# Layer 0's opening blocks in a hand-written order on four engines

## The chip, the cores and the metric

One core of one Trainium2 chip runs the whole program in one launch. The metric is the device time of one execution in microseconds (us). Matmuls run on TensorE (PE), elementwise work on VectorE (DVE), ScalarE (ACT) and GpSimd (POOL). Loads are issued by SyncE (SP) and carried out by the core's 16 DMA engines.

## The reference

Two layers of a bidirectional encoder over 2048 tokens of 1024 channels, then a final RMSNorm. What bears on the change is how a layer begins:

```python
h = rms_norm(x, norm_w[l])                 # x: (1, 2048, 1024), float32
proj = h @ w_in                            # one combined projection
qkv, z_a, a_lg, b_lg, cf_val, cf_glu, z_b, gate_lg = jnp.split(proj, pts, axis=-1)
qkv = jax.nn.silu(depthwise_conv_centred(qkv, qkv_conv_w))   # width 5
# q, k, v: 4 heads of 128; l2-normalised q and k; a_lg, b_lg: decay and write strength
# chunked delta rule forward and backward, gated norm, w_dn_out
# conformer branch: GLU, conv of width 31, layer norm, w_cf_out
# merge by gates, w_out, residual add
```

For the first layer, `rms_norm(x)` must be computed from the input itself: the sum of squares of each token over 1024 channels, its reciprocal root, and the scaled x.

## The kernel before, in words

Everything is kept channel-major: a tile has 128 channels on the partitions and tokens along the free axis. The 1024 channels are 8 tiles (index k, `KD`), and the 2048 tokens are four blocks of 512 (`NB`), two to a half. A product is made at high precision from rounded parts: an operand is split into a high half (`hi`, rounded, by ScalarE) and a low half (`lo`, the rest, by VectorE; `split`, L157 and L158). A column tile of 128 output channels over one block takes, for each k, three matmuls of 128x512: w high by h high, w high by h low, w low by h high (`dense_steps`, L174 to L176). The 16 columns for decay and write strength ("scalar tile") are stacked as high and low in one stationary tile `wab` and take two matmuls for each k (L408, L409).

The code is written for a planner: instructions are recorded in program order with their data dependencies, and the planner then chooses an order for each engine, and on which buffers an instruction waits, from its own model of times. In two cases the order is written by hand instead: `bind(start)` chains all instructions recorded since `start` on PE, ACT, DVE and POOL, each to the one before it on its engine. Before the change this is done for the delta rule's stage. DMA issues on SyncE are never bound.

Buffers come from pools of few slots: `big` (4), `mid` (3), `hm` (5), staging tiles `st` of 128x512 (3), weights `whi` and `wlo` (2 each), raw weights `wraw` (2 pieces of 4 k), PSUM `pd` (3 banks) and `pz` (5 banks). A new tile in a pool waits until an older one has been used up.

The opening of layer 0 is `head(0)`. It makes the scalar tile and the column tiles of k and q for head 0 (`conv_tiles([4, 0], block)`), block by block, while the generator `first_norm` is pulled along in small steps (`need`, `step_lead`). `first_norm` does, for each block: load 8 tiles of x, square them on ScalarE (L308), add them up (L310; VectorE for block 0, GpSimd for the others), sum over the partitions by four matmuls of one column (`token_sum`, L200), a reciprocal root by 11 small VectorE operations (L190 to L196), spread the factor over the partitions with diagonals and matmuls (`spread`, L206 and L208), and then, for each k, scale x (L327) and split it into the halves of h (L157, L158). Block 3 is loaded twice, the first time through staging tiles for the squares alone. Each column tile is copied from PSUM into a padded tile `cin` (L529), and after two blocks a depthwise convolution of width 5 runs over it: one ScalarE operation (L551) and four VectorE operations (L553) on some 1022 tokens, then SiLU (L540). After the opening come the scalars' chain (`scalars`), the v tile of head 0 (`conv_tiles([8])`), the conformer's tiles and the later heads.

Of the kernel before, what the change touches and what calls it, by code (L numbers as in the profile page):

```python
# [6 lines left out]
F32 = mybir.dt.float32  # L7
# [7 lines left out]
P = 128  # L15
# [20 lines left out]
R2 = 3.7  # L36
BIG = -1.0e30
# [39 lines left out]
class Trunk:  # L77
# [82 lines left out]
    def weight(self, src, kk):  # L160
        hi = self.pw.tile([P, KD, P], F32R, tag="whi", bufs=2, name="whi")[:, 0:kk, :]
        lo = self.pw.tile([P, KD, P], F32R, tag="wlo", bufs=2, name="wlo")[:, 0:kk, :]
        for k in range(0, kk, 4):
            raw = self.pw.tile([P, 4, P], F32, tag="wraw", bufs=2, name="wraw")
            self.load(raw, src[:, k:k + 4, :])
            self.split(hi[:, k:k + 4, :], lo[:, k:k + 4, :], raw)
# [35 lines left out]

    def spread(self, ps, r, n):
# [24 lines left out]
    def normalise(self, half, xn, r, wcol):  # L228
        nc = self.nc
        hs = [self.big([P, 2, KD, NB], F32R, f"h{2 * half + b}") for b in range(2)]  # L230
# [6 lines left out]
        for k in range(KD):  # L237
            for b in range(2):
# [4 lines left out]
                self.split(hs[b][:, 0, k, :], hs[b][:, 1, k, :], t)  # L243
# [4 lines left out]
    def run(self):  # L248
        tc, nc, a = self.tc, self.nc, self.a
        with tc.tile_pool(name="cst", bufs=1) as cst, \  # L250
# [26 lines left out]
            self.ready = 0  # L277
            h = [None] * 4
            self.h = h
            self.scalar_weights(0)  # L280
            self.lead = self.first_norm(a)
            next(self.lead)
# [4 lines left out]
    def first_norm(self, a):  # L287
        nc = self.nc
        stage = self.big([P, 2, KD, NB], F32, "x0")
        for blk in range(4):  # L290
            half, b = divmod(blk, 2)
            self.h[blk] = self.big([P, 2, KD, NB], F32R, f"h{blk}")
            hi, lo = self.h[blk][:, 0], self.h[blk][:, 1]
            src = [a["x"][k, :, blk * NB:(blk + 1) * NB] for k in range(KD)]
            if half == 0:
                x = [stage[:, b, k, :] for k in range(KD)]
            elif b == 0:
                x = self.first_tiles()
            if blk < 3:
                for k in range(KD):  # L300
                    self.load(x[k], src[k])
            acc = self.st("sqa")
            eng = nc.gpsimd if blk else nc.vector
            for k in range(KD):
                sq = self.st("sq0") if k else acc
                if blk == 3:
                    self.load(sq, src[k])
                nc.scalar.activation(sq, sq if blk == 3 else x[k], AF.Square)  # L308
                if k:
                    eng.tensor_tensor(out=acc, in0=acc, in1=sq, op=ALU.add)  # L310
            yield
            ps = self.pz()
            self.token_sum(ps, acc, 4)
            v = self.sm(4, "nv")
            r = self.sm(4, "nr")
            nc.vector.tensor_scalar(out=v, in0=ps[:, 0:4], scalar1=1.0 / D, scalar2=EPS,
                                    op0=ALU.mult, op1=ALU.add)
            self.rsqrt(r, v, 4)
            yield
            if blk == 3:  # L320
                x = self.first_tiles()
                for k in range(KD):
                    self.load(x[k], src[k])
            pr = self.pz()
            self.spread(pr, r, 4)
            for k in range(KD):
                nc.vector.scalar_tensor_tensor(out=x[k], in0=x[k], scalar=self.vec[:, V_NW + k:V_NW + k + 1], in1=pr,  # L327
                                               op0=ALU.mult, op1=ALU.mult)
                self.split(hi[:, k, :], lo[:, k, :], x[k])
                if k == KD - 1:  # L330
                    self.ready = blk + 1
                if k % 2:
                    yield

    def first_tiles(self):
        t = self.mid("x0m")
# [6 lines left out]
    def need(self, blk):  # L343
        while self.ready <= blk:
            next(self.lead)
# [1027 lines left out]
```

## Time and profile before

| | us |
|---|---|
| median of 3 runs | 3189.29 (3188.14 to 3192.9) |
| the profiled execution's own time | 3187.47 |
| its span | 3185.7 |
| TensorE busy | 3090.6 (97%) |
| VectorE busy | 2398.4 (75%) |
| ScalarE busy | 1385.3 (43%) |
| GpSimd busy | 302.3 (9%) |
| mean granted TensorE clock | 0.993 |

The span runs from the first to the last instruction of the profiled execution, and times in the timeline count from its start. In a row of the timeline the first number is the start, the second the duration, then engine, line, operation, output<-inputs and the count of merged instructions; in brackets stands how long the engine had been idle, and what released it. In a table of windows the columns are the window, its length, busy time and instruction counts of PE, PE's weight loads, DVE, ACT and POOL, the granted clock, the DMA engines' busy share and GB/s. A matmul's recorded duration overlaps the next one's, so the pace is read from start to start.

### The profile page before, as it was taken

What the parts mean: (1) busy time and instruction counts of PE and PEld (TensorE: products, weight loads), DVE (VectorE), ACT (ScalarE), POOL (GpSimd) and SP (SyncE); (2) the same over time, 40 slices, a digit from 0 to 9 for tenths busy, and PEclk for the clock granted to TensorE, in tenths of its full rate; (3) what the DMA queues carried; (4) which work ended last, traced back from release to release, by engine and by line L of the source; (5) the groups of instructions that cost most, each with busy time, mean ns of one, the idle gap of its engine ahead of it and who ended that gap; (6) DMA issues with size and microseconds to landing.
All of it is one profiled execution on the core that took longest, in us unless ns stands there. A gap on an engine that the chain in (4) does not pass through costs nothing. (4 is left out here: it accounts for less than half of the span.)

```text
span 3185.7 us, 51259 instructions
## 1 busy us (share of the span) xinstructions
PE 3090.6 (97%) x19110; PEld 2705.8 (85%) x19110; DVE 2398.4 (75%) x4409; ACT 1385.3 (43%) x3104; POOL 302.3 (9%) x297
## 2 busy tenths in 40 slices
PE   6999999999999999999999999999999999999997
PEld 5788888888889998787888888888888999878786
DVE  7789898987646697745676989898955567867655
ACT  5625151522444466533345242425234445655332
POOL 3000000000122231000000000000002222200000
PEclk9999999999999999999999999999999999999999
DMA  4323222334687886654413131414357777855634
GB/s 141 90 96 93 87 93 87 93 112 133 206 288 247 258 267 208 198 185 133 135 53 101 66 120 60 120 60 123 117 186 261 243 252 255 283 182 192 204 126 146
DMA packets 427545, 501.70 MB, mean 157 GB/s; under 512 B 96224, under 2 KB 260704, under 8 KB 427296
## 3 DMA queue, kind: packets, MB, share of 16 engines
q1 hardware_dynamic: 354544, 388.58, 39.2%
q10 hardware_dynamic: 64688, 80.09, 7.3%
q0 software_dynamic: 8064, 29.76, 2.5%
q8 instruction: 150, 2.46, 0.3%
q14 instruction: 99, 0.81, 0.1%
HBM read 342.74 MB, written 155.58 MB: 156 GB/s over the span
## 5 line engine op out<-in xcount | busy, mean ns | idle before, releaser
L174 PE MATMUL pd<-h,whi 128*128 128x512 f32 x2816 | 1092.1, 388 | 0.0
L176 PE MATMUL pd<-h,wlo 128*128 128x512 f32 x2816 | 1070.4, 380 | 1.9 <-DVE wlo L158 1.9
L175 PE MATMUL pd<-h,whi 128*128 128x512 f32 x2816 | 1070.9, 380 | 0.0
L728 DVE SCALAR_TENSOR_TENSOR cacc<-gp,vec,cacc 128x1009 f32<-128x1009 f32 (+1 forms) x480 | 614.3, 1280 | 37.5 <-ACT cacc L726 34.3
L176 PEld LDWEIGHTS pd<-h,wlo 128*128 128x128 f32 x2816 | 533.8, 190 | 79.3 <-DVE wlo L158 3.5
L174 PEld LDWEIGHTS pd<-h,whi 128*128 128x128 f32 x2816 | 534.0, 190 | 79.0 <-issue 1.4
L175 PEld LDWEIGHTS pd<-h,whi 128*128 128x128 f32 x2816 | 534.5, 190 | 72.4 <-issue 1.9
L157 ACT ACTIVATE whi<-wraw 128x512 fp32r<-128x512 f32 x400 | 242.7, 623 | 473.2 <-PE pd L175 335.9
L158 DVE TENSOR_TENSOR wlo<-wraw,whi 128x512 fp32r<-128x512 f32 x400 | 275.0, 701 | 142.1 <-ACT whi L157 141.8
L553 DVE SCALAR_TENSOR_TENSOR acc<-cin,vec,acc 128x1022 f32<-128x1022 f32 (+1 forms) x192 | 246.5, 1299 | 14.4 <-ACT acc L551 13.2
L176 PE MATMUL pd<-yhi,wlo 128*128 128x512 f32 x512 | 194.9, 381 | 3.8 <-DVE wlo L158 3.7
L174 PE MATMUL pd<-yhi,whi 128*128 128x512 f32 x512 | 194.6, 380 | 0.9 <-ACT whi L157 0.9
L175 PE MATMUL pd<-ylo,whi 128*128 128x512 f32 x512 | 194.0, 379 | 0.0
L808 ACT ACTIVATE go<-pd,vec 128x512 f32<-128x512 f32 x128 | 87.1, 680 | 147.9 <-PE pd L176 138.2
L529 ACT ACTIVATE cin<-pd 128x512 f32<-128x512 f32 x96 | 57.0, 594 | 154.7 <-PE pd L176 154.6
L176 PEld LDWEIGHTS pd<-yhi,wlo 128*128 128x128 f32 x512 | 96.8, 189 | 19.9 <-DVE wlo L158 6.4
L740 ACT ACTIVATE ao<-pd 128x512 f32<-128x512 f32 x64 | 38.3, 598 | 170.0 <-PE pd L176 169.9
L174 PEld LDWEIGHTS pd<-yhi,whi 128*128 128x128 f32 x512 | 96.8, 189 | 15.4 <-ACT whi L157 2.0
L175 PEld LDWEIGHTS pd<-ylo,whi 128*128 128x128 f32 x512 | 96.8, 189 | 13.6
L174 PE MATMUL pd<-uop,whi 128*128 128x512 f32 x256 | 101.0, 395 | 6.6 <-ACT whi L157 6.5
L176 PE MATMUL pd<-uop,wlo 128*128 128x512 f32 x256 | 99.1, 387 | 2.3 <-DVE wlo L158 1.4
L175 PE MATMUL pd<-gop,whi 128*128 128x512 f32 x256 | 97.7, 381 | 3.0 <-DVE gop L158 3.0
(297 smaller groups left out, 4754.9 us busy)
## 6 DMA issues: line engine op xcount, KB each, us to landing
wraw<-w_in SPq DMA_DIRECT2D x240, 256.0 KB, 3.3
gt<-go ACTq DMA_DIRECT2D x128, 256.0 KB, 3.6
dl<-gr SPq DMA_DIRECT2D x128, 256.0 KB, 5.2
dl<-kq SPq DMA_DIRECT2D x64, 512.0 KB, 6.1
dl<-kv SPq DMA_DIRECT2D x64, 512.0 KB, 5.8
wraw<-w_out SPq DMA_DIRECT2D x96, 256.0 KB, 3.0
kq<-acc SPq DMA_DIRECT2D x16, 1024.0 KB, 5.5
gr<-go ACTq DMA_DIRECT2D x64, 256.0 KB, 2.2
```

The lines of the kernel that those rows point to most:

```text
L157: self.nc.scalar.activation(hi, src, AF.Copy)
L158: self.nc.vector.tensor_tensor(out=lo, in0=src, in1=hi.bitcast(F32), op=ALU.subtract)
L174: mm(ps, whi[:, k, :], xhi, start=k == 0, stop=False)
L175: mm(ps, whi[:, k, :], xlo, start=False, stop=False)
L176: mm(ps, wlo[:, k, :], xhi, start=False, stop=k == kk - 1)
L529: nc.scalar.activation(cut(t[:, o + b * NB:o + (b + 1) * NB]), sort(ps), AF.Copy)
L553: self.nc.vector.scalar_tensor_tensor(out=out, in0=t[:, k:k + n], scalar=wc(k), in1=out, op0=ALU.mult, op1=ALU.add)
L728: self.nc.vector.scalar_tensor_tensor(out=acc, in0=t[:, k:k + n], scalar=wc(k), in1=acc, op0=ALU.mult, op1=ALU.add)
L740: nc.scalar.activation(cut(o), sort(ps), func)
L808: nc.scalar.activation(cut(o), sort(ps), AF.Identity, bias=self.vec[:, V_GB + j:V_GB + j + 1])
```

## The change

A new method `opening()` takes the place of `first_norm`, `scalar_tiles` and `conv_tiles([4, 0])` in layer 0; layer 1 is as before. All 32 tiles of x are loaded at once into tiles of their own, with the weights of k and q between them. The weights and `wab` are rounded on VectorE instead of ScalarE. The squares of blocks 0 and 1 are summed in PSUM, by token sums that accumulate (`token_add`): in block 0, pairs are added on VectorE first for k up to 5, and tiles 6 and 7 go straight to TensorE; in block 1 all eight go straight to TensorE. Squares of blocks 2 and 3 are added on GpSimd. The squares of later blocks are dealt out one for each k (`FIRST`). For each k of a block, x is scaled and split, and then the two matmuls of the scalar tile and the three of k and of q follow. The first-half convolutions are laid into block 3, one step for each k. All of it up to the last transposes is bound to the written order; the second-half convolutions follow unbound.

The core of the diff (the removed `first_norm` and `first_tiles` are not shown, nor the call sites' plumbing):

```diff
+FIRST = {1: (0, 0), 2: (0, 3), 3: (1, 0)}
-    def weight(self, src, kk):
+    def weight(self, src, kk, vector=False):
...
+            if vector:
+                self.nc.vector.tensor_scalar(out=hi[:, k:k + 4, :], in0=raw, scalar1=1.0, scalar2=None, op0=ALU.mult)
+                self.nc.vector.tensor_tensor(out=lo[:, k:k + 4, :], in0=raw, in1=hi[:, k:k + 4, :].bitcast(F32),
+                                             op=ALU.subtract)
+            else:
+                self.split(hi[:, k:k + 4, :], lo[:, k:k + 4, :], raw)
+    def token_add(self, ps, src, n, first, last):
+        for i in range(n):
+            self.nc.tensor.matmul(ps[:, i:i + 1], src[:, i * P:(i + 1) * P], self.ones[:, 0:1],
+                                  start=first and i == 0, stop=last, skip_group_check=True)
+    def opening(self):
...
+        start = self.mark()
...
+        self.scalar_weights(0, True)
+        fetch(0)
+        ws = [self.weight(a["w_in"][0, cols[0]], KD, True)]
+        fetch(1)
+        ws.append(self.weight(a["w_in"][0, cols[1]], KD, True))
+        fetch(2)
+        fetch(3)
...
+        def square(b, k):
+            sq = self.st("sqa") if k == 0 and b > 1 else self.st("sq0")
+            nc.scalar.activation(sq, xs[b][k], AF.Square)
+            if b < 2:
+                if k == 0:
+                    sums[b] = self.pz()
+                if b or k > 5:
+                    self.token_add(sums[b], sq, 4, k == 0, k == KD - 1)
+                elif k % 2:
+                    v_.tensor_tensor(out=acc[b], in0=acc[b], in1=sq, op=ALU.add)
+                    self.token_add(sums[b], acc[b], 4, k == 1, False)
+                else:
+                    acc[b] = sq
+            elif k:
+                nc.gpsimd.tensor_tensor(out=acc[b], in0=acc[b], in1=sq, op=ALU.add)
+            else:
+                acc[b] = sq
+        def factor(b):
+            if b > 1:
+                sums[b] = self.pz()
+                self.token_sum(sums[b], acc[b], 4)
...
+            self.rsqrt(r, v, 4)
+            return r
...
+        for k in range(KD):
+            square(0, k)
+        for k in range(3):
+            square(1, k)
+        r = factor(0)
+        later = deque([(1, k) for k in range(3, KD)] + [(2, k) for k in range(KD)] + [(3, k) for k in range(KD)])
+        for b in range(4):
...
+            self.spread(pr, r, 4)
+            if b == 0:
+                square(*later.popleft())
+                square(*later.popleft())
+            pss = [self.pd() for _ in range(3)]
+            for k in range(KD):
+                x = xs[b][k]
+                v_.scalar_tensor_tensor(out=x, in0=x, scalar=self.vec[:, V_NW + k:V_NW + k + 1], in1=pr,
+                                        op0=ALU.mult, op1=ALU.mult)
+                self.split(hi[:, k, :], lo[:, k, :], x)
+                xhi, xlo = mix(hi[:, k, :]), mix(lo[:, k, :])
+                mm(pss[0], self.wab[:, k, :], xhi, start=k == 0, stop=False)
+                mm(pss[0], self.wab[:, k, :], xlo, start=False, stop=k == KD - 1)
+                for ps, (whi, wlo) in zip(pss[1:], ws):
+                    mm(ps, whi[:, k, :], xhi, start=k == 0, stop=False)
+                    mm(ps, whi[:, k, :], xlo, start=False, stop=False)
+                    mm(ps, wlo[:, k, :], xhi, start=False, stop=k == KD - 1)
+                if later and (b, k) >= FIRST[later[0][0]]:
+                    square(*later.popleft())
+                if b == 3 and k == 4:
+                    begin(1)
+                if conv:
+                    if next(conv[0], None) is None:
+                        conv.popleft()
+                if k == 3 and turn:
+                    turned()
+                if k == 5 and b < 3:
+                    r = factor(b + 1)
+            ab = self.st("ab")
+            nc.scalar.activation(cut(ab[0:32, :]), sort(pss[0][0:32, :]), AF.Copy)
+            turn.append((b, ab))
+            for i, ps in enumerate(pss[1:]):
...
+                nc.scalar.activation(cut(t[:, o:o + NB]), sort(ps), AF.Copy)
...
+            if b == 2:
+                begin(0)
+        turned()
+        self.bind(start)
...
         if hd == 0:
-            block, pt = self.scalar_tiles()
-            kt, qt = self.conv_tiles([4, 0], block)
+            if self.l:
+                block, pt = self.scalar_tiles()
+                kt, qt = self.conv_tiles([4, 0], block)
+            else:
+                (kt, qt), pt = self.opening()
             self.post.append(self.scalars(pt))
```

`begin(i)` starts the convolution of tile i (its ScalarE operation), `turned()` transposes a block's scalar tile into token-major form, and `factor(b)` makes a block's reciprocal root.

More of the change, by code (lines that the diff above doesn't have):

```diff
@@ L229, in normalise @@
         nc = self.nc
-        hs = [self.big([P, 2, KD, NB], F32R, f"h{2 * half + b}") for b in range(2)]
+        ts = [self.big([P, 2, KD, NB], F32R, f"h{2 * half + b}") for b in range(2)]
+        hs = [(t[:, 0], t[:, 1]) for t in ts]
         self.nh[2 * half:2 * half + 2] = hs
```

135 lines of the change are left out of this document (68 added, 67 removed).

## The prediction

> **What bounds the kernel now.** I read the stages first (busy time by window), then TensorE's chain of waits, then the timeline of the opening. TensorE is busy for 97% of the span, but not in the opening. The last column tile of the first four blocks is evicted at 111.21; up to there the stages show:
> ```profile
> 0.00:111.10 111.10, 79.06 (x338) 63.45 (x339) 84.46 (x163) 58.35 (x94) 32.34 (x27) 0.94 0.37 118
> 111.10:200.00 88.90, 87.94 (x466) 78.06 (x465) 63.25 (x121) 51.72 (x120) 7.16 (x10) 1.00 0.35 102
> ```
> The first number behind the stage is its length, the next TensorE's busy time: 32 us idle in the first stage, 1 us in the second. After 111 TensorE is the bound, so whatever the opening gains or loses reaches the end nearly in full. In it TensorE waits for the first norm and for the pair of high and low halves:
> ```profile
> PE pz L200 <- DVE sqa L310: 13.4, 1, 13.4
> PE pd L408 <- ACT h L157: 5.2, 4, 1.5
> ```
> ```profile
> 20.59 0.75 DVE L327 SCALAR_TENSOR_TENSOR x<-x,vec,pz 128x512 f32<-128x512 f32 x1 [0.52 <-PE pz L208]
> 21.37 0.63 ACT L157 ACTIVATE h<-x 128x512 fp32r<-128x512 f32 x1 [0.15 <-DVE x L327]
> 111.21 0.58 ACT L529 ACTIVATE cin<-pd 128x512 f32<-128x512 f32 x1
> ```
> So the part that the change replaces has two marks: the first scaling of x at 20.6, and the end of the opening's matmuls at 111.1. My sum gives the same two marks for the new opening. Its base is the profiled execution, 3187.47 us (span 3185.7); the median of the runs, 3189.29, is 1.8 above it.
>
> **The change, part 1: the start.** The binding makes each of the four compute engines follow the written order from wab's split to the last transpose. On VectorE this order is: wab, k's weight split, q's weight split, and only then the first add of squares for block 0. On SyncE's queue q's weight follows x's blocks 0 and 1 and k's weight, as 19th and 20th piece of 262 KB.
> ```profile
> 2.00:8.00 6.00, 0.00 (x0) 0.00 (x0) 1.20 (x3) 4.21 (x6) 0.00 (x0) 1.00 0.92 289
> 8.00:14.00 6.00, 0.57 (x3) 0.57 (x3) 4.56 (x8) 4.67 (x8) 0.00 (x0) 1.00 1.00 371
> ```
> ```profile
> 1.19 4.46 SPq L145 DMA_DIRECT2D x<-x  x8
> 6.33 0.89 SPq L145 DMA_DIRECT2D wraw<-w_in  x2
> 7.26 3.16 SPq L145 DMA_DIRECT2D x<-x  x4
> ```
> The last column of the first fence is GB/s. With constants and wab (0.44 MB) the 20th piece ends 5.69 MB into the stream: 1.78 MB by 8.0, the other 3.91 MB at some 375 GB/s take 10.4 us, so it lands at 18.4. That all 32 pieces of x are asked for at once costs nothing beyond that: SyncE issues one in 0.56 (4.46 / 8), the transfer takes 0.7, and nothing else stands on its queue until the opening is over. Rounding to the high half on VectorE is not in the trace; a tensor-scalar takes 0.22 at 128 columns and 0.29 at 256, a two-input op 0.69 at 512:
> ```profile
> 37.04 0.87 DVE L206 TENSOR_SCALAR dg<-con,nr 128x128 f32<-128x128 f32 x4
> 108.07 0.29 DVE L465 TENSOR_SCALAR tri<-con 128x256 f32<-128x256 f32 x1
> ```
> I take 0.43, the line through the two (bounds 0.29 and 0.69). The last piece: 0.43 + 0.69, so VectorE is free for the squares at 19.6. ScalarE has done three squares by then and no more, since the three staging buffers are full. What follows is a chain with these prices:
> ```profile
> 9.50 3.88 DVE L310 TENSOR_TENSOR sqa<-sqa,sq 128x512 f32<-128x512 f32 x5 [1.02 <-ACT sq L308]
> 13.43 1.87 PE L200 MATMUL pz<-con,sqa 128*128 128x1 f32 x8 [13.43 <-DVE sqa L310]
> 84.85 1.05 PE L200 MATMUL pz<-con,sqa 128*128 128x1 f32 x8 [0.22 <-POOL sqa L310]
> 85.77 0.46 PE L175 MATMUL pd<-h,whi 128*128 128x512 f32 x1
> 15.34 0.16 DVE L316 TENSOR_SCALAR nv<-pz 128x4 f32<-128x4 f32 x1 [0.76 <-PE pz L200]
> 17.58 1.89 DVE L206 TENSOR_SCALAR dg<-con,nr 128x128 f32<-128x128 f32 x4
> ```
> An add takes 0.77, a token sum 1.87 on a cold TensorE and 0.92 (85.77 - 84.85) on a warm one, the reciprocal root 2.24 (15.34 to 17.58). Add, square, add, square, add, with squares 4 to 7 held back by buffers that token sums free: the third add ends at 24.5; five token sums (three of adds, two of single squares) end at 28.0 when they warm up on the way. Root: 30.2. The diagonals and their spread, 1.4 to 3.0 (20.59 - 17.58): first scaling at 32.0 instead of 20.6. Bounds: 29 (data 1 us earlier, all sums warm) and 36 (all cold).
>
> **Part 2: the loop over k.** In before, the planner lets one scaling run ahead. Now VectorE has scale(k), low(k), scale(k+1), and low(k) needs ScalarE's high(k):
> ```profile
> 32.28 0.68 DVE L158 TENSOR_TENSOR h<-x,h 128x512 fp32r<-128x512 f32 x1
> 32.88 0.73 DVE L327 SCALAR_TENSOR_TENSOR x<-x,vec,pz 128x512 f32<-128x512 f32 x1
> 33.65 0.63 ACT L157 ACTIVATE h<-x 128x512 fp32r<-128x512 f32 x1 [0.63 <-DVE x L327]
> 34.32 0.69 DVE L158 TENSOR_TENSOR h<-x,h 128x512 fp32r<-128x512 f32 x1
> 44.19 0.38 PE L174 MATMUL pd<-h,whi 128*128 128x512 f32 x1
> 44.40 0.38 PE L175 MATMUL pd<-h,whi 128*128 128x512 f32 x1
> ```
> From start to start: scale to high 0.77, high to low 0.67, low to scale 0.60, a period of 2.04. TensorE's eight matmuls of a k take 8 x 0.215 = 1.72, so they fit in and the chain of three sets the pace: 16.3 per block. ScalarE's square (0.63) fits beside its high half. Block 1's last five token sums, 0.92 each, are new on TensorE: two fall into the wait for the first high half, three put it 1.8 behind the chain, which it regains while VectorE works out the next factor; without that cover they cost 1.8.
>
> **Part 3: between the blocks.** The spread of the next block stands behind all matmuls of this one on TensorE, so nothing overlaps:
> ```profile
> 41.35 1.05 PE L208 MATMUL pz<-dg,con 128*128 128x128 f32 x8
> 42.44 2.06 DVE L327 SCALAR_TENSOR_TENSOR x<-x,vec,pz 128x512 f32<-128x512 f32 x3 [4.53 <-PE pz L208]
> ```
> From the last low: 0.69, seven matmuls 1.5, spread 1.09, with hand-over 3.4 instead of 0.6: 2.8 more, three times. The next block's scalar-tile evictions on ScalarE end before its first high half, and cost nothing; if they were late they would cost 0.6 each. The factor for the next block stands at k = 5. In block 0 its sums are ready: 2.2. In blocks 1 and 2 its token sum stands on TensorE behind the matmuls of k = 5, and VectorE's whole queue, the next scaling too, waits: 1.5 + 0.9 and hand-over, then 2.24, together 5.0 each.
>
> **Part 4: block 3.** One convolution step lies behind each low half; nothing of it lies in the wait for the high half, since that wait is ahead of it in the queue:
> ```profile
> 112.71 2.48 DVE L553 SCALAR_TENSOR_TENSOR acc<-cin,vec,acc 128x1026 f32<-128x1026 f32 x2
> 107.33 1.14 ACT L551 ACTIVATE acc<-cin,vec 128x1026 f32<-128x1026 f32 x1
> ```
> A step costs 1.2, the period 3.24. At k = 4 the second tile's scaling on ScalarE (1.14) delays its first step by 0.5. To the end of the matmuls: 7 x 3.24 + 0.5 + 1.44 + 2.3 = 26.9.
>
> **Part 5: smaller terms.** GpSimd's adds beside the low halves:
> ```profile
> L158 DVE TENSOR_TENSOR h<-x,h 128x512 fp32r<-128x512 f32 x8 | 8.4, 1090 | 0.5 <-ACT h L157 0.4
> L158 DVE TENSOR_TENSOR h<-x0h,h 128x512 fp32r<-128x512 f32 x4 | 2.6, 688 | 0.0
> ```
> The first row is the block of before during which GpSimd adds, the second the one without: 0.4 more each. Fourteen adds lie in blocks 0 to 2; 0 to 5.6, and I take 2.0, since each mostly falls between two lows. Three staging buffers shared by squares, diagonals and scalar tiles: 0 to 2, I take 0.5. Then TensorE's clock:
> ```profile
> 52.91 1.27 PE L200 MATMUL pz<-con,sqa 128*128 128x1 f32 x8 [2.39 <-POOL sqa L310]
> 55.03 0.63 PE L175 MATMUL pd<-h,whi 128*128 128x512 f32 x1
> 55.46 0.63 PE L176 MATMUL pd<-h,wlo 128*128 128x512 f32 x1
> 82.06 0.43 PE L414 MATMUL pz<-con,ab 32*128 32x32 f32 x4 [2.50 <-ACT ab L411]
> 82.42 0.48 PE L175 MATMUL pd<-h,whi 128*128 128x512 f32 x1
> ```
> After an idle time of 2.39 matmuls start every 0.43 instead of 0.215; after one of 2.50 they don't. The new gaps (about 4 at each of two factors, 2 at each block's start) may cost 0 to 5; I take 1.5, because half of a slow stretch hides in the chain's slack. The Trainium skill (TensorE: Matmul & The Clock Gate, "What's actually happening") says that the clock halves after an idle window of about 3.4 us and comes back after as long a busy one. By that rule the two factor gaps alone would cost an estimated 3.4 us instead of my 1.5.
>
> **Part 6: behind the opening.** v's weights were split while q's last block ran; now both weight buffers are held to the last k. TensorE waits for one high half and its hand-over, 1.2 (0 to 2). The scalars' chain on VectorE now starts with both second-half convolutions behind the opening, some 3 us later against TensorE than before; it is already waited for:
> ```profile
> 105.80 0.63 ACT L157 ACTIVATE whi<-wraw 128x512 fp32r<-128x512 f32 x1
> 127.78 0.43 PE L466 MATMUL pz<-abw,tri 128*128 128x64 f32 x2 [0.96 <-DVE abw L456]
> ```
> That is 1.0 more (0 to 3). What the change removes (splits on ScalarE, the late loads of block 3, GpSimd's adds for block 1) was cover or wait inside the 111 us and has no price of its own.
>
> **The sum.** 32.0 + (16.3 + 2.2 + 2.8) + 2 x (16.3 + 5.0 + 2.8) + 26.9 + 2.0 + 0.5 + 1.5 = 132.4 for the end of the opening's matmuls, against 111.1: 21.3 later. With 2.2 behind it, 23.5: 3187.5 + 23.5 = 3211. All low ends: 29 + 96.4 = 125.4, 14.3 later, 3202. All high ends: 36 + 96.4 + 5.6 + 2 + 5 + 2 + 3 less 111.1 = 38.9, 3226.
>
> **The rivals.** *The engines don't follow the written order* (faster): the planner keeps its freedom, adds go ahead of q's split and a scaling runs ahead of each low half, as in before. Then the start stays at 20.6 and TensorE is the bound of every block: four times 13.8 + 2.8 and five sums of 0.92 in block 0 end at 91.6. That is 19.5 earlier; with 2.2 behind, 3170. For it: in before that pace of VectorE exists (scalings and lows in turn without waiting, 32.28 to 34.32). Against it: the same binding is used in the delta stage of before, and there VectorE does sit idle with written work behind the waiting one (the steps at L995):
> ```profile
> 1010.88 0.28 DVE L929 COPY dh<-pz 32x128 f32<-32x128 f32 x1 [5.37 <-ACT dm L985]
> ```
> It decides if the opening ends before 109. The Trainium skill (the same page, "Engine queue depths") calls VectorE's queue strictly first in, first out; so nothing passes a waiting low half once the order is fixed.
>
> *Late start, but TensorE-bound blocks* (the same): the chain of scale, high and low overlaps more than the rows show, the factor hides, and only the start is lost: 32.0 + 66.4 + 6 for the steps of block 3 that don't fit = 104 to 110, with 2.2 behind, between 5 earlier and 1 later: 3187. For it: 1.72 against 2.04 is a small distance. Against it: a queue in order gives no overlap between a low and the scaling behind it.
>
> **How the numbers follow.** A difference of 0.2%, 6.4 us, is about what runs of this kernel can tell from none. The forecast, 3202 to 3226, holds 0.74, all of it slower by over 0.2%. The free order holds 0.14, faster. The third holds 0.12, within 0.2%. The range, 3186 to 3225, takes in the forecast and half of the third case. The predicted time is the forecast's, 3211.
>
> **What would show it.** In the changed profile: VectorE's first add of squares behind q's two splits, near 19.6; first scaling near 32; scalings 2.04 apart in blocks 0 to 2 and 3.24 in block 3; scaling gaps of 5 to 6 after k = 5 in blocks 1 and 2; last eviction of a column tile near 132; busy windows behind it like those behind 111 before. Scalings under 1.8 apart or a first scaling before 26 would make it wrong.

## The result, and the profile after

The changed kernel takes 3230.31 us (median of 4 runs, 3227.78 to 3234.7); the kernel before, timed beside it, 3191.1 (4 runs). The ratio is 1.0118 with a 95% interval of 1.0106 to 1.013: slower by 39 us, where the prediction said 21.7 over the median it was made against. The time lies above the prediction's range (3186 to 3225) and above the forecast's bounds (3202 to 3226). The profiled execution took 3227.78 with a span of 3226.0, 40.3 above the span before.

The stages first, as two windows of the changed kernel, cut where its opening ends and 88.9 further on:
```profile
0.00:140.30 140.30, 97.46 (x421) 78.09 (x421) 74.10 (x160) 50.68 (x82) 18.25 (x20) 0.96 0.21 75
140.30:229.20 88.90, 84.19 (x441) 74.05 (x441) 59.30 (x119) 49.22 (x120) 6.09 (x8) 0.98 0.36 103
```
The first stage is 29.2 longer and holds 43 us of idle TensorE instead of 32. The second, busy all but 1 us before, now has 4.7 us of idle time. TensorE's waits in the first 160 us name the places:
```profile
PE pz L211 <- DVE sq L338: 22.3, 2, 22.0
PE pd L390 <- ACT h L158: 17.2, 12, 3.6
PE pd L182 <- DVE wlo L159: 3.5, 1, 3.5
```
The first token sum waits for VectorE until 22.0, where it waited until 13.4 before; the high halves are waited for 17.2 in all, where it was 5.2; the third line lies behind the opening.

VectorE's timeline shows the start and the pace of the blocks:
```profile
20.65 0.69 DVE L169 TENSOR_TENSOR wlo<-wraw,whi 128x512 fp32r<-128x512 f32 x1
21.26 0.68 DVE L338 TENSOR_TENSOR sq<-sq,sq 128x512 f32<-128x512 f32 x1
...
31.15 0.16 DVE L353 TENSOR_SCALAR nv<-pz 128x4 f32<-128x4 f32 x1 [5.37 <-PE pz L211]
...
38.19 0.75 DVE L386 SCALAR_TENSOR_TENSOR x<-x,vec,pz 128x512 f32<-128x512 f32 x1 [3.82 <-PE pz L219]
...
61.26 0.75 DVE L386 SCALAR_TENSOR_TENSOR x<-x,vec,pz 128x512 f32<-128x512 f32 x1 [0.67 <-PE pz L219]
...
63.31 0.74 DVE L386 SCALAR_TENSOR_TENSOR x<-x,vec,pz 128x512 f32<-128x512 f32 x1
...
77.01 0.16 DVE L353 TENSOR_SCALAR nv<-pz 128x4 f32<-128x4 f32 x1 [2.65 <-PE pz L206]
...
112.96 0.75 DVE L386 SCALAR_TENSOR_TENSOR x3a<-x3a,vec,pz 128x512 f32<-128x512 f32 x1 [2.66 <-PE pz L219]
...
116.21 0.74 DVE L386 SCALAR_TENSOR_TENSOR x3a<-x3a,vec,pz 128x512 f32<-128x512 f32 x1
```
The first add of squares stands right behind the last piece of q's split, as the written order has it. The first scaling comes at 38.2 instead of 20.6. The blocks begin at 38.2, 61.3, 88.0 and 113.0. Within a block scalings follow each other at 2.05 (61.26 to 63.31), in block 3 at 3.25 (112.96 to 116.21).

TensorE's timeline shows what lies between 21.3 and 38.2:
```profile
22.00 3.58 PE L211 MATMUL pz<-con,sq 128*128 128x1 f32 x16 [22.00 <-DVE sq L338]
25.83 10.40 PE L211 MATMUL pz<-con,sq 128*128 128x1 f32 x48 [0.26 <-DVE sq L338]
36.10 2.06 PE L219 MATMUL pz<-dg,con 128*128 128x128 f32 x8
...
41.22 0.78 PE L390 MATMUL pd<-h,wab 128*128 128x512 f32 x1
...
44.77 1.03 PE L211 MATMUL pz<-con,sq 128*128 128x1 f32 x8
```
Ten groups of eight passes ran nearly without a break for 19 us, and each took 1.7 to 1.8; none reached the 0.92 of a warm TensorE. The first five are block 0's; three of block 1 stand behind them, and the spread of block 0's factor (36.10) only behind those. Only after 3.5 us of matmuls of 512 columns (from 41.22), which start every 0.43 until then, does a group take about 1.

Behind the opening, VectorE and TensorE:
```profile
143.14 9.67 DVE L650 SCALAR_TENSOR_TENSOR acc<-cin,vec,acc 128x1026 f32<-128x1026 f32 x8 [2.25 <-ACT acc L647]
152.73 0.69 DVE L159 TENSOR_TENSOR wlo<-wraw,whi 128x512 fp32r<-128x512 f32 x1
```
```profile
139.94 0.38 PE L395 MATMUL pd<-h,wlo 128*128 128x512 f32 x1
...
153.47 0.48 PE L182 MATMUL pd<-h,wlo 128*128 128x512 f32 x1 [3.52 <-DVE wlo L159]
```
The opening's matmuls end at 140.3 (139.94 and 0.38), 29.2 later than the prediction's mark of before, 111.1. v's second low half then stands behind eight convolution steps, and TensorE waits 3.5 for it.

How the delay travels to the end can be read from the starts of two groups, the conformer's `glu` and the delta rule's products with `dm` (duration min, median, max in ns; first and last start). Before, then after:
```profile
L713 ACT ACTIVATE glu<-pd x32: 578/597/605, 144.5 to 2210.6; 128x512 f32<-128x512 f32 x32
L1001 PE MATMUL pz<-dm,dl x512: 273/275/377, 925.3 to 2825.7; 128*128 128x128 f32 x171
```
```profile
L813 ACT ACTIVATE glu<-pd x32: 577/597/604, 180.1 to 2249.0; 128x512 f32<-128x512 f32 x32
L1101 PE MATMUL pz<-dm,dl x512: 272/275/377, 961.0 to 2861.7; 128*128 128x128 f32 x171
```
The delay is 35.6 at the first `glu`, 35.7 at the first product with `dm`, 36.0 at the last one, and 40.3 at the end. So it divides into 17.6 at the start, 11.6 in the blocks (29.2 at the opening's end), 6.4 just behind it, and 4.7 later, of which 4.3 arise in the last 364 us. That last stretch took 360.0 before and 364.3 after, and between 359.0 and 366.2 in the profiled executions of the first eight experiments below, which all leave its code alone. So the 4.3 are no larger than what the stretch varies by, and they aren't shown to come from the change.

### The profile page after: what moved, and what is told of

The parts are those of the page before. It is cut to its first block, busy times and chain, and to the rows that moved or that the text cites. A ratio compares the mean times of both kernels' runs of the same rounds, so it can differ in the third digit from the quotient of the medians.

```text
span 3226.0 us, 51376 instructions
## 1 busy us (share of the span) xinstructions
PE 3115.0 (97%) x19198; PEld 2726.2 (85%) x19198; DVE 2395.0 (74%) x4411; ACT 1373.8 (43%) x3093; POOL 288.0 (9%) x290
## 5 line engine op out<-in xcount | busy, mean ns | idle before, releaser
L180 PE MATMUL pd<-h,whi 128*128 128x512 f32 x2752 | 1065.9, 387 | 0.0
L182 PE MATMUL pd<-h,wlo 128*128 128x512 f32 x2752 | 1045.6, 380 | 5.1 <-DVE wlo L159 5.1
L181 PE MATMUL pd<-h,whi 128*128 128x512 f32 x2752 | 1044.6, 380 | 0.0
L182 PEld LDWEIGHTS pd<-h,wlo 128*128 128x128 f32 x2752 | 521.4, 189 | 80.3 <-DVE wlo L159 7.4
L180 PEld LDWEIGHTS pd<-h,whi 128*128 128x128 f32 x2752 | 521.0, 189 | 76.5 <-issue 1.2
L181 PEld LDWEIGHTS pd<-h,whi 128*128 128x128 f32 x2752 | 521.4, 189 | 69.9 <-issue 1.9
L1321 ACT ACTIVATE gt<-gt 128x512 f32<-128x512 f32 (+1 forms) x64 | 53.9, 843 | 111.3 <-DMA gt<-gt 105.6
```

The source lines that it names most:

```text
L180: mm(ps, whi[:, k, :], xhi, start=k == 0, stop=False)
L181: mm(ps, whi[:, k, :], xlo, start=False, stop=False)
L182: mm(ps, wlo[:, k, :], xhi, start=False, stop=k == kk - 1)
L1321: nc.scalar.activation(gt[:, 0:n], gt[:, 0:n], AF.Sigmoid)
```

## The experiments

Theory: the whole loss arises in and right behind the opening, from the bound order (late adds, a chain without overlap, v's weights late), made worse by a TensorE that one-column sums leave cold. Rivals: the loss comes from the sums themselves wherever they stand; or from the later stages. Every ratio below is to the kernel before, timed together with the experiment. The times of one kernel lie up to 13 us apart (3186.71 to 3199.9 for the kernel before in one set), so a difference of some 5 us between the medians of two experiments isn't clear of noise; marks within the opening are read from the traces. Code is cut at `...` and in places drawn together; remarks behind `#` are not in the kernels.

**The order unbound** (`e_unbound`). The same instructions, the planner free to order them.
```diff
         turned()
-        self.bind(start)
```


> The changed kernel without the binding of its opening: the same operations, the planner chooses their order. Theory (the written order costs the time: q's split ahead of the first sums, scale and low in turn, factors and spreads behind matmuls): the first scaling comes near 23 us instead of 38.2, the opening's matmuls end between 98 and 112 instead of 140, and the time is 3185 us (3172 to 3200). Rival (the new work itself costs it: sums on TensorE, rounding on VectorE, all loads at once): first scaling after 33, time 3222 or more.

3200.8 us (10 runs), ratio 1.0024 (1.0014 to 1.0033), span 3201.2. VectorE, then TensorE's waits up to 130:
```profile
7.85 0.69 DVE L338 TENSOR_TENSOR sq<-sq,sq 128x512 f32<-128x512 f32 x1 [3.28 <-ACT sq L331]
...
17.75 0.16 DVE L353 TENSOR_SCALAR nv<-pz 128x4 f32<-128x4 f32 x1 [5.04 <-PE pz L211]
```
```profile
PE pd L182 <- DVE wlo L159: 5.8, 1, 5.8
PE pd L180 <- ACT whi L158: 5.0, 1, 5.0
```
About 30 of the 39 us go, so the binding is their cause. The first add moves from 21.3 to 7.9, ahead of both splits, and the first scaling to 24.8. The opening's matmuls end at 108.7, 2.4 earlier than in the kernel before. But the first `glu` comes at 156.4, 11.9 later than there: right behind the opening TensorE waits 10.8 for v's weights (the two waits), and its matmuls run at half pace behind each. This was missing from the expectation, whose upper edge the time just exceeds.

**Scaling one k ahead** (`e_ahead`). The scaling of k+1 is written ahead of the low half of k; the order stays bound.
```diff
-                v_.scalar_tensor_tensor(out=x, ...)          # scale(k)
-                self.split(hi[:, k, :], lo[:, k, :], x)
+                nc.scalar.activation(hi[:, k, :], x, AF.Copy)
+                if k + 1 < KD:
+                    scale(k + 1)
+                v_.tensor_tensor(out=lo[:, k, :], in0=x, in1=hi[:, k, :].bitcast(F32), op=ALU.subtract)
```


> Changed kernel, bound as before, but the scaling of k+1 is written ahead of the low half of k. Theory (scale, high and low in turn set the pace of 2.05 us per k): blocks 0 to 2 run at TensorE's 1.72 per k, block 3 at VectorE's 2.46; the opening ends some 17 us earlier, near 123, and the time is 3213 us (3208 to 3219). Rival (TensorE or the buffers set the pace): under 4 us gained, 3226 or more.

3218.36 us, ratio 1.0074 (1.0057 to 1.0091). Block 3 of its VectorE timeline:
```profile
117.15 0.74 DVE L385 SCALAR_TENSOR_TENSOR x3a<-x3a,vec,pz 128x512 f32<-128x512 f32 x1
117.81 0.68 DVE L394 TENSOR_TENSOR h<-x3a,h 128x512 fp32r<-128x512 f32 x1
...
119.61 0.74 DVE L385 SCALAR_TENSOR_TENSOR x3a<-x3a,vec,pz 128x512 f32<-128x512 f32 x1
```
In block 3 no wait for the high half is left, and the period falls from 3.25 to 2.46. But blocks 0 to 2 together are no shorter (first scalings at 37.8 and, in block 3, 113.9). The wait moves there: in block 0 VectorE waits 2.98 and 3.40 for high halves, in block 2 4.14 for the factor instead of 2.66, and 4.41 at the boundary to block 3 instead of 2.66. The opening ends only 5.9 earlier, where 17 were expected. The time lies within the expectation (3208 to 3219) all the same, but by luck: the profiled execution is only 2.9 shorter than that of the changed kernel.

**q's split behind the squares** (`e_q_late`). The two rounding pairs of q's weights are emitted behind the last square ahead of the loop.
```diff
-        ws.append(self.weight(a["w_in"][0, cols[1]], KD, True))
+        wq, halves = self.weight_parts(a["w_in"][0, cols[1]], KD)   # loads now, splits when called
+        ws.append(wq)
...
             square(1, k)
+        halves()
         r = factor(0)
```


> Changed kernel, bound, but q's weight is split on VectorE behind the sums of squares and ahead of the first factor. Theory (the first add waits for q's split): first add near 14.7 instead of 21.3, first scaling near 31.6 instead of 38.2, 6.6 us gained: 3224 us (3220 to 3227). Rival (the sums on TensorE alone set the start): first scaling after 36, under 2 us gained.

3221.79 us, ratio 1.0089 (1.0074 to 1.0104).
```profile
31.02 0.75 DVE L404 SCALAR_TENSOR_TENSOR x<-x,vec,pz 128x512 f32<-128x512 f32 x1 [3.82 <-PE pz L235]
```
The start is 7.2 earlier: of its 17.6, 7.2 are q's split. Only 3.5 of them are left at the opening's end. In block 0 matmuls now run at half pace for 8.7 us (34.04 to 42.72) instead of 3.5, with a group of one-column sums among them, and a high half stands on ScalarE behind a square that waits for such a sum; VectorE waits 2.95 for it. The median is 8.5 lower, the profiled execution only 3.6.

**v's weights ahead of the second-half convolutions** (`e_v_first`).
```diff
         self.bind(start)
+        self.early = [self.weight(a["w_in"][0, 8], KD)]     # used by conv_tiles([8])
         while conv:
```


> Changed kernel, bound, but v's weights are asked for and split in program order ahead of the second-half convolutions. Theory (VectorE's eight convolution steps stand ahead of v's second low half, TensorE waits 3.5 us and then runs 3.4 us at half speed): that gap at 150 to 153.5 is gone, 5 to 6 us gained: 3225 us (3222 to 3228). Rival (the loss behind the opening is the order of later work): gap gone, but under 2 us gained at the end.

3239.95 us, ratio 1.0147 (1.0132 to 1.0162): 10 slower than the changed kernel. TensorE's wait for v is gone, and the first `glu` starts 5.6 earlier. But the planner put a later instruction, the one on `sol`, elsewhere. ScalarE's row and TensorE's waits from 200 to 300, where TensorE has none in the changed kernel:
```profile
237.24 1.06 ACT L783 ACTIVATE sol<-sol 128x1024 f32<-128x1024 f32 x1 [15.16 <-POOL sol L781]
```
```profile
PE pd L183 <- DVE wlo L160: 5.5, 1, 5.5
PE pd L181 <- ACT ao L843: 4.9, 1, 4.9
```
ScalarE waits 15.2 for a GpSimd result with the evictions `ao` behind it, and TensorE runs dry twice, 10.4 in all. The first product with `dm` comes 10.7 later than in the changed kernel (971.7 against 961.0). So a local gain can be lost to the planner's later order. Of the 6.4 behind the opening, the 5.6 are confirmed as v's weights.

**Wide token sums** (`e_wide`). The accumulating sums multiply by 128 columns of ones instead of one.
```diff
-            self.nc.tensor.matmul(ps[:, i:i + 1], src[:, i * P:(i + 1) * P], self.ones[:, 0:1],
+            self.nc.tensor.matmul(ps[:, i * P:(i + 1) * P], src[:, i * P:(i + 1) * P], self.ones,
```


> The token sums that accumulate get 128 columns of ones instead of one, everything else as in the changed kernel. Question: why did 19 us of token sums, nearly back to back, run at the cold pace (1.79 for a group of eight passes) and not speed up. Theory one, narrow matmuls don't speed TensorE up because they keep it too little busy: with 128 columns the sums begin at 2.06 each and fall to about 1.05 after some 4 us, so the first factor's reciprocal root starts near 28 instead of 31.15 and the first scaling near 32 instead of 38.2; time about 3224. Theory two, it is the instruction (float32, or its waits), not the width: the sums stay at about 2.06 each, root near 33, first scaling near 41; time about 3233.

3221.36 us, ratio 1.0092 (1.0077 to 1.0107).
```profile
21.84 9.76 PE L211 MATMUL pz<-con,sq 128*128 128x128 f32 x64 [21.84 <-DVE sq L338]
31.64 1.16 PE L219 MATMUL pz<-dg,con 128*128 128x128 f32 x8
```
```profile
32.84 0.75 DVE L387 SCALAR_TENSOR_TENSOR x<-x,vec,pz 128x512 f32<-128x512 f32 x1 [0.66 <-PE pz L219]
```
More work, and faster: eight groups in 9.76 instead of 13.98, the spread in 1.16 instead of 2.06, the first scaling at 32.8 instead of 38.2. Width decides, as theory one had it. The opening ends 4.6 earlier.

**A TensorE at speed ahead of the narrow sums** (`e_warm`). 72 matmuls of 512 columns, whose result nothing reads, ahead of the first sum.
```diff
+        pw = self.pz()
+        for _ in range(72):
+            mm(pw, self.wab[:, 0, :], self.wab[:, 0:4, :].rearrange("p k c -> p (k c)"), start=True, stop=True)
         for k in range(KD):
             square(0, k)
```


> The changed kernel with 72 extra matmuls of 128x512 on the rounded scalar tile, whose result nothing reads, ahead of the first token sum, in TensorE's idle time from about 4.5 to 22. The token sums keep one column. Question: do sums of one column keep a TensorE at speed that is at speed already. Theory one, a sum of one column counts as idle: the first two to four groups run at 0.92, then the pace falls back to 1.79; the first root near 29 to 30, first scaling near 36 (38.2 without), time about 3228. Theory two, it counts as work once the clock is up: all groups run at 0.92, the root starts near 28, the first scaling near 32, as the prediction had it, time about 3224.

3236.45 us, ratio 1.0134 (1.0112 to 1.0157).
```profile
4.58 18.17 PE L370 MATMUL pz<-wab 128*128 128x512 f32 x72 [4.58 <-DVE wab L490]
22.59 1.93 PE L211 MATMUL pz<-con,sq 128*128 128x1 f32 x16
25.50 10.40 PE L211 MATMUL pz<-con,sq 128*128 128x1 f32 x48 [0.98 <-DVE sq L338]
```
Two groups run at 0.96, then all six at 1.73: theory one, and the first scaling is at 37.9. In this run the record of the granted clock shows it as well: 1.00 from 4.5 to 22.5, 0.50 from 25.5 to 41. The time is worse than expected. The opening ends 2.7 later than in the changed kernel; 1.7 of it are there at the start of block 1 (63.0 instead of 61.3), behind a block 0 whose matmuls run at half pace until 48.7 instead of 44.8. The rest of the 6 between the medians is not placed, and with four runs 12 us apart it isn't clear of noise.

**Squares added on VectorE and GpSimd** (`e_adds`). One token sum for each block, as in the kernel before.
```diff
-            if b < 2:
-                ...                                   # token_add for every square or pair
-            elif k:
-                nc.gpsimd.tensor_tensor(out=acc[b], ...)
+            if k:
+                (nc.gpsimd if b else v_).tensor_tensor(out=acc[b], in0=acc[b], in1=sq, op=ALU.add)
```


> Undoes one part: squares of block 0 are added on VectorE and of block 1 on GpSimd, with one token sum for each block, as in the kernel before; q's weight split stays ahead of them and the order stays bound. Theory one, the PSUM sums on a cold TensorE are a part of the late start of their own: seven adds of 0.77 from 21.3 end at 26.7, one sum 1.87, root 2.24, diagonals and spread 3.0 with no block-1 sums in the way: first scaling at 34 instead of 38.2. Block 0 loses five sums of 0.92 and gains a wait of 2.6 for the factor of block 1. Opening 5 us shorter, time 3225 (3221 to 3228). Theory two, the start is set by q's split alone and the sums hide behind something else: first scaling stays near 38, time 3230 to 3233.

3226.83 us, ratio 1.0108 (1.0091 to 1.0125).
```profile
28.19 0.16 DVE L343 TENSOR_SCALAR nv<-pz 128x4 f32<-128x4 f32 x1 [1.96 <-PE pz L206]
...
32.54 1.89 DVE L217 TENSOR_SCALAR dg<-con,nr 128x128 f32<-128x128 f32 x4
35.32 0.75 DVE L376 SCALAR_TENSOR_TENSOR x<-x,vec,pz 128x512 f32<-128x512 f32 x1 [0.89 <-PE pz L219]
```
The sums end 3.0 earlier, but the root takes 4.35 (28.19 to 32.54) instead of 2.35, two of its operations taking 1.2 instead of 0.16 while block 1's adds run on GpSimd (more of that below). Of the 2.9 gained at the start only 0.7 are left at block 3, since block 1's factor is now waited for in block 0 (2.66). The gain at the start is 1.3 smaller than expected, and the opening gets 0.7 shorter, not 5. That the time lies within the expectation is luck: its 3.5 below the changed kernel isn't clear of noise.

**Factor and spread ahead of the matmuls they stood behind** (`e_factor`).
```diff
+                if k == 4 and 0 < b < 3:
+                    total(b + 1)                  # token sum, was behind k = 5
+                if k == 7 and b < 3:
+                    self.spread(nextpr, r, 4)     # was behind k = 7
                 mm(pss[0], ...)
```


> Undoes the waits between the blocks, as the changed kernel otherwise is: the token sum for the next factor goes ahead of the matmuls of k = 4 instead of behind those of k = 5, and the next block's diagonals and spread go ahead of the matmuls of k = 7 instead of behind them. Theory one, the prediction's prices hold: 2.6 at each of two factors and 2.6 at each of three boundaries go, 13.0 together, less 0.9 of diagonals that still lie on VectorE: opening 10 to 13 shorter, 3219 (3216 to 3223). Theory two, the waits shift instead of going (TensorE is behind by the time, as when the scaling ran ahead and the opening got only 5.9 shorter): opening 3 to 6 shorter, 3225.

3224.91 us, ratio 1.0108 (1.0089 to 1.0127). The beginning of block 3 on VectorE:
```profile
106.28 0.75 DVE L390 SCALAR_TENSOR_TENSOR x3a<-x3a,vec,pz 128x512 f32<-128x512 f32 x1 [0.49 <-PE pz L219]
110.19 0.69 DVE L159 TENSOR_TENSOR h<-x3a,h 128x512 fp32r<-128x512 f32 x1 [3.16 <-ACT h L158]
```
And ScalarE at the same place:
```profile
106.72 0.59 ACT L417 ACTIVATE ab<-pd 32x512 f32<-32x512 f32 x1 [2.60 <-PE pd L400]
...
109.54 0.62 ACT L158 ACTIVATE h<-x3a 128x512 fp32r<-128x512 f32 x1
```
Theory two. The scaling waits 0.49 instead of 2.66, but the first high half stands on ScalarE behind the three evictions, which wait for the last matmuls (and, in block 3, behind the convolution's first operation): 3.16 of the same wait, one engine on. The opening got 4.2 shorter, not 13. The two factor waits did go: from the scaling of k = 5 to that of k = 6 it takes 5.78 and 4.17 in blocks 1 and 2, instead of 7.65 and 6.91. The boundaries gave nothing.

**All repairs together** (`e_best`): VectorE adds block 0's squares ahead of both splits, GpSimd those of blocks 1 to 3; q's weights are loaded ahead of block 1; scaling and high half run one k ahead over the boundaries (so the high half stands ahead of the evictions); the factor is made in pieces from k = 3, the spread ahead of k = 6; no convolution step inside block 3; and q's tile of block 3 comes last, over v's weights:
```diff
+                if k == 6 and b < 3:
+                    spread(b + 1)
+                scale(*nxt); low(b, k); high(*nxt)      # nxt: (b, k + 1) or (b + 1, 0)
...
+        self.early = [self.weight(a["w_in"][0, 8], KD)]
+        for k in range(KD):
+            tile(pss[2], wq, 3, k)                      # q's tile of block 3
```


> All four repairs together, still in a bound order: squares of block 0 added on VectorE ahead of both weight splits with one token sum; squares of blocks 1 to 3 on GpSimd; q's weights asked for ahead of block 1 of x; each scaling and high half one k ahead of the low half; the next factor's sum at k = 3, its root in pieces, its spread ahead of k = 6; no convolution steps inside block 3; v's weights requested before q's tile of block 3, whose 24 matmuls come last and cover them. Theory one, the opening's parts add up: first scaling at 19 instead of 38.2, blocks of 16 to 17.5 with a cold first one 5 longer, opening's matmuls end near 93 instead of 139.9 (before 110.7). All of it reaches the end: 3192 - 18 = 3174 (3165 to 3183). Theory two, TensorE's cold clock and the planner's later order take most of it back, as with v's weights alone (first glu 5.6 earlier, the end 10 later): 3185 to 3200.

3183.85 us, ratio 0.9973 (0.9961 to 0.9984). The opening ends at 102.2 and the first `glu` is 9.4 earlier than before, half of what was expected; the time lies just outside theory one's range. VectorE shows one reason:
```profile
16.20 1.27 DVE L373 SCALAR_TENSOR_TENSOR nr<-rst,nr 128x4 f32<-128x4 f32 x1
...
17.70 1.12 DVE L372 TENSOR_TENSOR rst<-rst,nr 128x4 f32<-128x4 f32 x1
...
24.07 0.75 DVE L391 SCALAR_TENSOR_TENSOR x<-x,vec,pz 128x512 f32<-128x512 f32 x1 [0.52 <-PE pz L220]
```
```profile
16.19 5.30 POOL L355 TENSOR_TENSOR sqa<-sqa,sq 128x512 f32<-128x512 f32 x4 [15.22 <-ACT sq L351]
```
Four of the root's operations take 1.1 to 1.3 instead of 0.16, one for each of four GpSimd adds of 1.3, and the first scaling is at 24.1 where 19 was expected.

Extra wide matmuls alone on top of this (`e_best_w`):

> e_best with 32 such extra matmuls ahead of the first token sum, four behind it and four behind the first spread. In e_best TensorE ran block 0 cold until 32.9. Theory one, the extra matmuls bring the clock up before the first block and the gaps of 6.7 in between are too long to hold it: first scaling unchanged at 24, block 0 still cold, 3184. Theory two, the clock holds over the gaps: block 0 some 4 shorter, 3180.

3188.36 us, ratio 0.9985 (0.9976 to 0.9995). The first scaling stays at 23.9, as theory one had it. The opening ends 1.7 earlier, but the time shows no gain: if anything it is 4 slower.

**`e_best2`**: extra matmuls ahead of the first sum, and block 1's squares summed by wide matmuls instead of on GpSimd (the squares of later blocks are dealt out a little later to suit).
```diff
+        warm(32)                                        # as in e_warm
...
+            if b == 1:
+                for i in range(4):
+                    mm(sums[1][:, i * P:(i + 1) * P], sq[:, i * P:(i + 1) * P], self.ones, ...)
```


> e_best with 32 extra matmuls ahead of the first token sum, and block 1's squares summed in PSUM by matmuls with 128 columns of ones instead of adds on GpSimd. In e_best four of the twelve small operations of the first root took 1.1 to 1.3 instead of 0.16, each beside a GpSimd add, and block 0 ran cold until 32.9. Theory one, both costs go: root and diagonals in 3.1 instead of 7.2, first scaling at 20 instead of 24.1; the wide sums keep the clock up, so block 0 gains 3 to 4 more and gives back 3 for the three sums inside it; opening's last matmul 5 to 8 earlier, 3177 (3172 to 3182). Theory two, the small operations are slow for another reason or the wide sums delay the first spread: first scaling 22 to 24, 3184.

3179.68 us, ratio 0.9965 (0.995 to 0.998).
```profile
17.74 0.88 DVE L218 TENSOR_SCALAR dg<-con,nr 128x128 f32<-128x128 f32 x4 [0.18 <-PE pz L356]
...
20.36 0.75 DVE L397 SCALAR_TENSOR_TENSOR x<-x,vec,pz 128x512 f32<-128x512 f32 x1 [0.68 <-PE pz L220]
```
With GpSimd silent no operation of this root takes over 0.17, and the first scaling is at 20.4, as expected. The opening ends at 99.2, 3.0 earlier than in `e_best`, where 5 to 8 were expected. In this kernel both repairs were made at once, so their shares are not separated beyond the root's 3.9 (15.34 to 21.62 in `e_best`, 15.36 to 17.74 here).

**`e_best3`**: the factor's sum one k later, and its root no longer in pieces but whole behind k = 5 (the second edit is not shown).
```diff
-                if k == 3 and 0 < b < 3:
+                if k == 4 and 0 < b < 3:
                     total(b + 1)
```


> e_best2 with the token sum for the next factor one k later (k = 4) and its reciprocal root whole behind k = 5. In e_best2 TensorE waited 1.67 twice for the last GpSimd add ahead of that sum (at 48.7 and 68.2), and behind the second wait it ran at half pace until 72. Theory one, both waits and the slow stretch go: 5 earlier at the opening's end, 3175. Theory two, the whole root in one place on VectorE makes TensorE wait as long: 3180, as e_best2.

3176.87 us, ratio 0.9958 (0.9942 to 0.9975): 14 us faster than the kernel before and 53 faster than the changed one. The two waits for GpSimd are gone (the sum at 49.72 starts without one), and in their place TensorE waits for the next factor's diagonals, as theory two had it:
```profile
49.72 1.05 PE L207 MATMUL pz<-con,sqa 128*128 128x1 f32 x8
...
76.86 1.25 PE L220 MATMUL pz<-dg,con 128*128 128x128 f32 x8 [3.61 <-DVE dg L218]
```
Its opening ends at 99.8, where that of `e_best2` ended at 99.2, so the expected 5 us did not come. The 2.8 us between the two times aren't won in the opening, and they aren't clear of noise (the intervals overlap).

## Why the prediction was wrong

The direction and the mechanism held; the size did not: the profiled execution got 40.3 longer, where 23.5 was forecast. The step that failed is the price of the token sums in Part 1, "when they warm up on the way": one-column sums never warmed TensorE up. The other term that was off is Part 6. By steps:

- *Part 1, the start: failed.* Forecast 32.0 (bounds 29 and 36), measured 38.2, outside the bounds. The 6.2 divide as follows. The first add came 1.7 late (21.3, not 19.6): the first of q's two pieces was there at 19.13, and both were rounded behind it (2.1), where the forecast let the last one land at 18.4 and counted one (1.1). From the first add to the root it took 9.9 instead of 8.4, since five sums ran cold: 1.5. The root took 0.1 more. From the diagonals to the first scaling it took 4.7 instead of 1.8, since three sums of block 1, cold too, stand ahead of the spread: 2.9. For these three Part 1 has no term, and Part 2 counts only the last five of block 1. At the warm price of 0.92 they would have ended at some 30.8 and hidden behind root and diagonals; at 1.73 they ended at 36.1. So 4.4 of the 6.2 come from sums that stayed cold, and the bound "all cold" has no term for 2.9 of that either. The experiment with wide sums shows it: on the same order both terms come back to the forecast, 7.9 and 1.5, and the first scaling to 32.8.
- *Part 2, the loop: right.* 2.05 against 2.04. The rounding on VectorE, costed by a line between two rows, took 0.43, exactly as taken.
- *Part 3, the boundaries: right as a sum.* Waits of 2.65 for the two factors and of 2.6 for the spread at blocks 2 and 3; at block 1 it was 0.67, behind 1.23 of waiting for GpSimd. From the first scaling to the end of the matmuls: 100.4 forecast, with Part 5's 4.0, and 102.1 measured (38.2 to 140.3). But the terms of the boundaries can't be taken off: with factor and spread moved ahead, the opening gained 4.2, not 13. The factors gave what they cost, the boundaries nothing, because the evictions on ScalarE end the same wait.
- *Part 4, block 3: right.* 3.24 forecast, 3.25 measured; 26.9 forecast to the end of the matmuls, 27.3 measured (112.96 to 140.3).
- *Part 5, the clock:* the price of 1.5 for the gaps was of the right kind: the mean granted clock from 60 to 140 was 0.94, with 0.71 from 80 to 90 behind a factor's gap, and it was 1.00 throughout when the factor waits were taken away. The price itself was not measured by itself.
- *Part 6, behind the opening: mis-sized.* 2.2 forecast, 6.4 measured. The term "one high half and its hand-over" was looked for on ScalarE; the wait is for the second low half on VectorE, behind 9.7 us of convolution steps. In the kernel before, v's low halves stood ahead of these steps (at 106.46 and 107.46, the steps from 108.50). Behind its 3.5 of waiting TensorE also runs at half pace until 157. Requesting v's weights earlier took 5.6 of the 6.4 away.
- *Behind that:* 4.7 more up to the end, forecast as none. 4.3 of them lie in the last stretch, which varies by as much from execution to execution, so that no step of the prediction is shown to have failed there.

Together: 6.2 + 1.7 + 4.2 + 4.7 = 16.8 above the forecast's 23.5, the 40.3 of the profiled execution.

The rival "engines don't follow the written order" was rightly given little: they do, and removing the binding takes back 30 us. Its price of 3170 was wrong for the unbound kernel (3200.8): the opening's matmuls ended at 108.7 there, not at 91.6, and it had no term for v's weights behind them. The rival "TensorE-bound blocks" needed scalings 1.72 apart, and they were 2.05 apart.

## What to carry to other kernels

A written order is as good as its worst entry: a weight split that waits for the 20th transfer, put ahead of the adds, cost 7 us at the start, 3.5 of them still at the opening's end, because the adds behind it did not pass it though their data were there; write each engine's order by when the data arrive and by who waits behind. Where TensorE idles before its first real work, as here, a reduction over the partitions was better made with 128 columns than with one, though most of the result is thrown away. And when several waits lie one behind the other, taking one away shows the next: no single repair tried here brought the time below the kernel before; several together (early adds, overlap, early factor, wide sums, covered weights) turned 39 us of loss into 14 us of gain.

## What the runs showed of the hardware that was not expected

One-column matmuls did not count as work for TensorE's clock. In the changed kernel 80 passes of them in 19 us, nearly back to back, ran at half pace throughout. With a TensorE at speed they lost it within 3 us (0.96, 0.96, then 1.73 for a group), and the granted clock then stood at 0.50 through 10 us of them without a break. The same sums with 128 columns brought it up (`e_wide`):
```profile
36.64 1.05 PE L211 MATMUL pz<-con,sq 128*128 128x128 f32 x8
```
The Trainium skill (TensorE: Matmul & The Clock Gate, "What's actually happening") says that about 3.4 us of sustained activity bring the clock up whatever the number of matmuls. For matmuls of 512 columns this trace agrees (3.5 us from 41.22); for those of one column it does not. Where a group of one-column sums stood early among the matmuls of 512 columns at half pace, these took 8.7 us (`e_q_late`) and 7.8 us (`e_warm`) to come up.

The granted clock in the table of windows read 1.00 through all of the first 40 us of the changed kernel, while the durations say half: ahead of the first change in the record the durations are to be believed.

Small VectorE operations beside GpSimd are not a little slower but blocked: operations of 128x4 took 1.1 to 1.3 instead of 0.16, about as long as one GpSimd add of 1.3. It hits those with one tensor input too: one took 1.26 in `e_best3` (at 32.33, beside a GpSimd add from 32.27). The Trainium skill (SBUF — State Buffer, "Who interferes with whom") calls the port pair that the two engines share an exclusive lock; the rows of `e_best` agree, and the first root of `e_best2`, with GpSimd silent, has none above 0.17. For a chain of small operations the price was about one GpSimd instruction each time, not the 0.4 seen on operations of 0.69.
